# Layer 0's value projection: tile 0's values in front of tile 1's turning, and two engines kept in source order

## The chip, the cores and the metric

The kernel runs on one core of one Trainium2 chip. The metric is the device time of one execution in microseconds (us). Before the change it is 2489.64 us, the median of three runs from 2487.28 to 2490.44.

The engines are called as in the profile: PE is the tensor engine, ACT is ScalarE, DVE is VectorE, POOL is GpSimd, SP is the engine that issues the DMAs.

## The reference

A decoder trunk of two layers over 1024 tokens of width 1024, in float32: layer 0 mixes with native sparse attention (NSA), layer 1 with forgetting attention over shared keys and values. Each layer also attends to 256 memory tokens and ends with a gated convolutional FFN. What matters here is how layer 0 begins:

```python
def rms_norm(x, g):
    xf = x.astype(jnp.float32)
    y = xf * lax.rsqrt(jnp.mean(xf * xf, axis=-1, keepdims=True) + EPS)
    return (y * g.astype(jnp.float32)).astype(x.dtype)
...
h = rms_norm(x, attn_norm[l])
...
proj = h @ w_in
q = proj[..., :MIX_W].reshape(B, S, N_MIX_HEADS, HEAD_DIM)
kv = proj[..., MIX_W:MIX_W + BRANCH_KV_W].reshape(B, S, 6, N_KV_GROUPS, HEAD_DIM)
gate_logit = proj[..., MIX_W + BRANCH_KV_W:MIX_W + BRANCH_KV_W + GATE_W]
...
gates = jax.nn.sigmoid(gate_logit + gate_b).reshape(B, S, N_MIX_HEADS, 3)
```

The rows of x are normalized, and of their projection two value blocks (128 columns each) and the 36 gate columns are made first: 292 columns in all.

## The kernel before

Every float32 operand of a matmul is split into a high and a low half, and each product is made of three matmuls, high by high, high by low and low by high (`mm3`, lines 171 to 173). The halves are made by `split`: the high half by an ACT copy (line 86), the low half by a DVE subtraction (line 92).

`layer0_proj` holds the first part of layer 0. The 1024 tokens are 8 tiles of 128 rows. A tile goes through these steps:

- `load_x` (line 1183): a DMA of the 512 KB tile `xl`, into one of two buffers.
- `norm_x`: ACT squares the rows and sums them (line 132, it writes into `xn`), ACT makes the mean (line 127, `ss`), POOL the power -1/2 (line 135, `rs`), DVE the product with the gain `gb` (line 149, `xn`, two buffers).
- `norm_turn`: PE turns (transposes) eight blocks of 128x128 into two PSUM tiles `psb` (line 164), and both are split into `hT` (lines 86 and 92).
- the values: 24 matmuls of 292 columns over the 8 blocks of the depth (lines 171 to 173) into one `psb`, out of `hT` and the split weights `wh` and `wl`, of which there are four pairs with two depth blocks each. The fourth pair's raw weights `wr` have to wait for one of three buffers.
- `store_v`: the 256 value columns are split into `sv` (line 86 on ACT, line 92 on DVE) and stored to DRAM (line 272). DVE adds the gate bias (line 1203).

PSUM gives four `psb` tiles, shared by the turning and the values. Behind the eight tiles ACT makes the sigmoid of the gates (line 1204), and PE goes on to the projections of keys and queries, the compression of the keys and the memory tokens' keys and values, in an order that a string of letters sets.

A scheduler of the framework sets each engine's order: of the instructions whose inputs it believes ready it takes the one with the best priority, by estimates of its own. Under `tc.manual_schedule(engines=...)` the named engines keep the order in which the code issues the block's instructions, and instructions from outside the block can still go between. In the loop before, no engine is under it: the code norms and turns tile t+1 ahead of the values of tile t, and the scheduler orders all engines. On each engine the instructions then run strictly in the order of its queue.

Of the kernel before, what the change touches and what calls it, by code (L numbers as in the profile page):

```python
# [17 lines left out]
P = 128  # L18
D = 1024
S = 1024  # L20
NT = S // P
# [23 lines left out]
class Trunk:  # L45
# [1120 lines left out]
    def layer0_proj(self, cpool):  # L1166
        nc, a, tc = self.nc, self.a, self.tc
        w = a["a_w_in"][0]
        self.mem = []
        self.qd0 = self.dp.tile([2, 2, NH * 32, S], F32, name="qd0")  # L1170
        self.kd0 = self.dp.tile([2, 2, 4 * 32, S], F32, name="kd0")
        self.vd0 = self.dp.tile([S, 4, 2 * HD], F32, name="vd0")
        self.qm0 = self.dp.tile([2, NMH * HD, S], F32, name="qm0")
        self.gates = cpool.tile([P, NT, NH * 3], F32, name="gates")
        self.kc = cpool.tile([P, NG, 64], F32R, name="kc")
        self.vc = cpool.tile([P, NG, 2, HD], F32R, name="vc")
        with tc.tile_pool(name="l0p", bufs=1) as pool:
            h = [self.hpair() for _ in range(2)]
            xs = []

            def load_x(t):
                xs.append(self.sb(pool, [P, D], F32, "xl", 2))
                nc.sync.dma_start(xs[t], a["x"][0, t * P:(t + 1) * P, :])

            def norm(t):
                self.norm_t(pool, xs[t], gb, h[t // 4][0], h[t // 4][1], (t % 4) * P)
            load_x(0)
            gb = self.gain(pool, a["attn_norm"][0:1, :], 2)
            wv = self.load_block(w, [(1152, 128), (1408, 164)])
            gbias = pool.tile([P, NH * 3], F32, name="gbias")  # L1190
            nc.sync.dma_start(gbias, a["a_gate_b"].to_broadcast([P, NH * 3]))
            norm(0)
            for t in range(NT):
                if t + 1 < NT:
                    load_x(t + 1)
                    norm(t + 1)
                ps = self.psb()[:, 0:292]
                hh, hl = h[t // 4]
                o = (t % 4) * P
                for kt in range(KT):  # L1200
                    self.mm3(ps, (hh[:, kt, o:o + P], hl[:, kt, o:o + P]), wv(kt, 0, 292), kt == 0, kt == KT - 1)
                self.store_v(pool, ps[:, 0:256], self.vd0[t * P:(t + 1) * P], 4)
                nc.vector.tensor_tensor(self.gates[:, t, :], ps[:, 256:292], gbias, ALU.add)
            nc.scalar.activation(self.gates, self.gates, AF.Sigmoid)
            g0 = self.gates.rearrange("p t (h b) -> p t h b", b=3)[:, 0, :, 0]
            nc.vector.tensor_scalar(g0, g0, self.rv, None, ALU.mult)
            self.masks(pool, cpool)
            ct = pool.tile([P, 2, 32], F32, name="ct")
            nc.sync.dma_start(ct, a["rope_cmp"])
            comp = [self.compress(pool, h, w, kind, ct) for kind in range(2)]  # L1210
            mems = [self.mem_kv(pool, l) for l in range(2)]
            keys = self.rope_proj(cpool, h, w, [(1024, 128), (1280, 128)], self.kd0, 0, None)
            first = self.rope_proj(cpool, h, w, [(0, 256)], self.qd0, 0, QSC)
            order = "k cc kkk m kkk dd kkkk m kkk c kkk m d q m c q m c q m d q m d q n c q n d q n c q n d qq n qq n q n qqqqqq"
            gens = {"k": keys, "q": first, "c": comp[0], "d": comp[1], "m": mems[0], "n": mems[1]}
            for name in order.replace(" ", ""):
                next(gens[name], None)
            for g in (comp[0], comp[1], mems[0], mems[1], first):
                for _ in g:
                    pass  # L1220
        return h
# [1224 lines left out]
```

## Time and profile before

| | us |
|---|---|
| median of three runs | 2489.64 |
| the profiled execution | 2489.81 |
| its span | 2487.7 |
| PE busy in it | 2424.5 |
| first turning of tile 0, from the span's start | 8.17 |
| first value matmul | 18.86 |
| first turning of tile 7 | 43.93 |
| first matmul of the key projection | 51.23 |

The span is the time from the first to the last instruction that the profile shows. A row of a timeline gives the start and the length of an instruction (or of several equal ones, with their count), its engine and line, what it writes and reads, and in brackets how long the engine had been idle and what it waited for. Lengths of matmuls overlap, because they are pipelined: the distance between two starts is what one costs.

### The profile page before, as it was taken

What the parts mean: (1) busy time and instruction counts of PE and PEld (TensorE: products, weight loads), DVE (VectorE), ACT (ScalarE), POOL (GpSimd) and SP (SyncE); (2) the same over time, 40 slices, a digit from 0 to 9 for tenths busy, and PEclk for the clock granted to TensorE, in tenths of its full rate; (3) what the DMA queues carried; (4) which work ended last, traced back from release to release, by engine and by line L of the source; (5) the groups of instructions that cost most, each with busy time, mean ns of one, the idle gap of its engine ahead of it and who ended that gap; (6) DMA issues with size and microseconds to landing.
All of it is one profiled execution on the core that took longest, in us unless ns stands there. A gap on an engine that the chain in (4) does not pass through costs nothing.

```text
span 2487.7 us, 35535 instructions
## 1 busy us (share of the span) xinstructions
PE 2424.5 (97%) x12210; PEld 2041.9 (82%) x12210; DVE 1897.2 (76%) x3143; ACT 1362.4 (55%) x2623; POOL 744.1 (30%) x620
## 2 busy tenths in 40 slices
PE   7999999998999999999999999999999999999998
PEld 7788888877878888888889988887777888888886
DVE  5757999894598888788666478878479788788765
ACT  5435989894454444454455257757254444454444
POOL 0114455454165545520000000001236545451000
PEclk9999999999999999999999999999999999999999
DMA  8465233255423333366336567666613323338523
GB/s 253 144 207 161 70 87 101 82 144 168 161 73 110 106 102 110 101 240 227 102 119 186 156 178 202 187 181 190 214 68 111 106 94 114 98 102 318 167 93 120
DMA packets 303276, 357.68 MB, mean 144 GB/s; under 512 B 38024, under 2 KB 183288, under 8 KB 303096
## 3 DMA queue, kind: packets, MB, share of 16 engines
q1 hardware_dynamic: 303096, 355.41, 45.2%
q8 instruction: 97, 1.59, 0.3%
q14 instruction: 83, 0.68, 0.1%
HBM read 245.55 MB, written 109.78 MB: 143 GB/s over the span
## 4 chain that ended last, share of the span: by engine, by line
PE 81%; DVE 8%; ACT 3%; issue 3%; DMA 2%; POOL 1%; SPq 0%; POOLq 0%; DVEq 0%; ACTq 0%
PE psb L171 16%; PE psb L172 16%; PE psb L173 16%; PE psa L171 6%; PE psa L173 6%; PE psa L172 6%; PE psa L321 5%; PE psb L453 5%; PE psb L480 5%; DVE wl L92 1%; DVE hT L92 1%; DVE pt L467 1%; ACT ps L381 1%; ACT pt L464 1%; DVE ps L361 1%
## 5 line engine op out<-in xcount | busy, mean ns | idle before, releaser
L2056 DVE SCALAR_TENSOR_TENSOR v<-u,cw,v 128x1023 f32<-128x1023 f32 (+1 forms) x176 | 288.8, 1642 | 64.1 <-ACT v L2054 64.0
L92 DVE TENSOR_TENSOR wl<-wr,wh 128x512 fp32r<-128x512 f32 (+2 forms) x244 | 233.4, 961 | 117.6 <-ACT wh L86 117.1
L86 ACT ACTIVATE wh<-wr 128x512 fp32r<-128x512 f32 (+2 forms) x244 | 182.2, 751 | 241.4 <-PE psa L173 109.8
L171 PE MATMUL psb<-hT,wh 128*128 128x512 f32 x736 | 293.1, 398 | 0.4 <-DVE pt L467 0.4
L467 DVE TENSOR_TENSOR pt<-psb,pt 128x512 fp32r<-128x512 f32 (+2 forms) x380 | 247.5, 660 | 60.3 <-ACT pt L464 58.0
L173 PE MATMUL psb<-hT,wl 128*128 128x512 f32 x736 | 287.8, 391 | 0.0
L172 PE MATMUL psb<-hT,wh 128*128 128x512 f32 x736 | 287.6, 391 | 0.0
L464 ACT ACTIVATE pt<-psb 128x512 fp32r<-128x512 f32 (+2 forms) x380 | 216.1, 575 | 95.1 <-PE psb L453 91.9
L2054 ACT ACTIVATE v<-u,cw 128x1024 f32<-128x1024 f32 x88 | 109.6, 1246 | 285.2 <-DVE u L2043 273.8
L480 PE MATMUL psb<-pt,vv 128*128 128x512 f32 (+2 forms) x864 | 221.1, 356 | 5.6 <-DVE pt L467 4.7
L321 PE MATMUL psa<-kk,qq 128*128 128x512 f32 (+4 forms) x792 | 176.3, 340 | 5.0 <-ACT pm L378 3.0
L381 ACT ACTIVATE ps<-ps,stat 128x640 f32<-128x640 f32 (+4 forms) x192 | 147.8, 774 | 28.2 <-DVE stat L361 27.9
L173 PEld LDWEIGHTS psb<-hT,wl 128*128 128x128 f32 x736 | 138.3, 188 | 29.3
L135 POOL TENSOR_TENSOR rs<-ss,consts 128x1 f32<-128x1 f32 x24 | 17.3, 720 | 482.0 <-ACT ss L127 315.9
L171 PEld LDWEIGHTS psb<-hT,wh 128*128 128x128 f32 x736 | 138.5, 188 | 27.1 <-DVE pt L467 1.1
L172 PEld LDWEIGHTS psb<-hT,wh 128*128 128x128 f32 x736 | 138.6, 188 | 25.1
L453 PE MATMUL psb<-consts,ps 128*128 128x128 f32 x928 | 146.9, 276 | 7.3 <-DVE ps L419 2.8
L480 PEld LDWEIGHTS psb<-pt,vv 128*128 128x128 f32 x864 | 137.4, 192 | 19.7 <-DVE pt L467 7.5
L361 DVE CUSTOM_DVE_ANT_0 ps<-psa,caub 128x128 f32<-128x128 f32 (+1 forms) x192 | 139.7, 751 | 15.6 <-PE psa L321 13.8
L544 POOL TENSOR_TENSOR wr<-wr 128x512 f32<-128x512 f32 x16 | 21.8, 1368 | 408.6 <-DVE stat L361 240.4
L321 PEld LDWEIGHTS psa<-kk,qq 128*128 128x128 f32 x792 | 121.5, 189 | 24.3 <-DVE stat L361 5.3
L453 PEld LDWEIGHTS psb<-consts,ps 128*128 128x128 f32 x928 | 110.4, 142 | 34.0 <-DVE ps L419 4.6
(327 smaller groups left out, 6647.3 us busy)
## 6 DMA issues: line engine op xcount, KB each, us to landing
wr<-in_w_up_dram SPq DMA_DIRECT2D x88, 512.0 KB
wr<-gd SPq DMA_DIRECT2D x154, 256.0 KB
gd<-v SPq DMA_DIRECT2D x88, 256.0 KB
o<-ob SPq DMA_DIRECT2D x128, 128.0 KB
wr<-o SPq DMA_DIRECT2D x32, 512.0 KB
hT<-in_w_down_dram SPq DMA_DIRECT2D x64, 256.0 KB
gd<-gs SPq DMA_DIRECT2D x60, 256.0 KB
qd<-st SPq DMA_DIRECT2D x56, 256.0 KB
```

Source lines behind the costliest of these rows:

```text
L86: self.nc.scalar.activation(hi, src, AF.Copy)
L92: self.nc.vector.tensor_tensor(lo, src, f32(hi), ALU.subtract)
L171: mm(out, lh, rh, start=first, stop=False, skip_group_check=more)
L172: mm(out, lh, rl, start=False, stop=False, skip_group_check=more)
L173: mm(out, ll, rh, start=False, stop=last, skip_group_check=more)
L321: nc.tensor.matmul(out, w, rhs, start=b not in banks[:i], stop=b not in banks[i + 1:])
L381: nc.scalar.activation(p, p, AF.Exp, bias=st[:, 0, ii:ii + 1], scale=-1.0, accum_out=st[:, 1, ii:ii + 1])
L453: nc.tensor.transpose(tp[0:kb, x:x + P], br["pt"][ii][:, o:o + kb], self.ident)
L464: nc.scalar.activation(st["hi"], st["src"], AF.Copy)
L467: self.nc.vector.tensor_tensor(st["lo"], st["src"], f32(st["hi"]), ALU.subtract)
L480: self.nc.tensor.matmul(out, v, t, start=st["begin"] and i == 0, stop=st["end"] and i == len(mms) - 1)
L2056: nc.vector.scalar_tensor_tensor(v[:, d:], u[:, :S - d], cw[:, tap, i:i + 1], v[:, d:], ALU.mult, ALU.add)
```

## The change

The norm and the turning of a tile become two calls, and the loop is written out anew: tile 0 is turned, tile 1 is normed, tile 0's values are made, and only then tile 1 is turned. For tiles 2 to 7, tile t is loaded, normed and turned, and then the values of tile t-1 are made. The whole stands under `manual_schedule` for PE and ACT. DVE, POOL and SP stay with the scheduler.

```diff
-            def norm(t):
-                self.norm_t(pool, xs[t], gb, h[t // 4][0], h[t // 4][1], (t % 4) * P)
             load_x(0)
...
-            norm(0)
-            for t in range(NT):
-                if t + 1 < NT:
-                    load_x(t + 1)
-                    norm(t + 1)
+            def turn(t, xn):
+                self.norm_turn(xn, h[t // 4][0], h[t // 4][1], (t % 4) * P)
+
+            def values(t):
                 ps = self.psb()[:, 0:292]
...
+            with tc.manual_schedule(engines={mybir.EngineType.PE, mybir.EngineType.Activation}):
+                turn(0, self.norm_x(pool, xs[0], gb))
+                load_x(1)
+                xn = self.norm_x(pool, xs[1], gb)
+                values(0)
+                turn(1, xn)
+                for t in range(2, NT):
+                    load_x(t)
+                    turn(t, self.norm_x(pool, xs[t], gb))
+                    values(t - 1)
+                values(NT - 1)
```

PE at the start of the program, before. `xn_129` holds the normed rows of tile 0, `xn_152` those of tile 1; `psb_173` takes the values of tile 0:

```order
L164 MATMUL psb_136<-consts,xn_129 128x128 x4
L164 MATMUL psb_143<-consts,xn_129 128x128 x4
L164 MATMUL psb_159<-consts,xn_152 128x128 x4
L164 MATMUL psb_166<-consts,xn_152 128x128 x4
L171 MATMUL psb_173<-wh_102,hT_91 128x292
L172 MATMUL psb_173<-wl_103,hT_91 128x292
```

PE at the same place, after. `xn_131`, `xn_154` and `xn_207` are tiles 0, 1 and 2; `psb_161` takes the values of tile 0, `psb_228` those of tile 1:

```order
L164 MATMUL psb_138<-consts,xn_131 128x128 x4
L164 MATMUL psb_145<-consts,xn_131 128x128 x4
L171 MATMUL psb_161<-wh_102,hT_91 128x292
L172 MATMUL psb_161<-wl_103,hT_91 128x292
...
L173 MATMUL psb_161<-wh_123,hT_92 128x292
L164 MATMUL psb_191<-consts,xn_154 128x128 x4
L164 MATMUL psb_198<-consts,xn_154 128x128 x4
L164 MATMUL psb_214<-consts,xn_207 128x128 x4
L164 MATMUL psb_221<-consts,xn_207 128x128 x4
L171 MATMUL psb_228<-wh_102,hT_91 128x292
```

The 24 value matmuls of tile 0 moved ahead of the turning of tile 1. From the turning of tile 2 on, PE has the same sequence as before.

ACT in the rounds of tiles 1 to 3, before. `xn_258` and `xn_311` are the squares of tiles 3 and 4, `psb_159` and `psb_212` are turned blocks of tiles 1 and 2, and `sv_198` is the eviction of tile 0's values:

```order
L86 ACTIVATE hT_91<-psb_159 128x4x128
L86 ACTIVATE hT_91<-psb_166 128x4x128
L132 ACTIVATE xn_258,ss_259<-xl_256 128x1024
L127 ACTIVATE ss_259<-ss_259,eps 128x1
L86 ACTIVATE sv_198<-psb_173 128x4x64
L86 ACTIVATE hT_91<-psb_212 128x4x128
L86 ACTIVATE hT_91<-psb_219 128x4x128
L132 ACTIVATE xn_311,ss_312<-xl_309 128x1024
L127 ACTIVATE ss_312<-ss_312,eps 128x1
L86 ACTIVATE sv_251<-psb_226 128x4x64
```

ACT at the same place, after. `xn_207` and `xn_260` are the squares of tiles 2 and 3, `psb_191` and `psb_214` are turned blocks of tiles 1 and 2, and `sv_186` and `sv_253` are the evictions of the values of tiles 0 and 1:

```order
L86 ACTIVATE sv_186<-psb_161 128x4x64
L86 ACTIVATE hT_91<-psb_191 128x4x128
L86 ACTIVATE hT_91<-psb_198 128x4x128
L132 ACTIVATE xn_207,ss_208<-xl_205 128x1024
L127 ACTIVATE ss_208<-ss_208,eps 128x1
L86 ACTIVATE hT_91<-psb_214 128x4x128
L86 ACTIVATE hT_91<-psb_221 128x4x128
L86 ACTIVATE sv_253<-psb_228 128x4x64
L132 ACTIVATE xn_260,ss_261<-xl_258 128x1024
L127 ACTIVATE ss_261<-ss_261,eps 128x1
```

Before, the square of tile t+3 stands ahead of the eviction of tile t's values. After, the square of tile t+2 stands behind it.

On DVE the product of tile 1 moves ahead of the fourth weight's low half, and each later product behind the value eviction and gate sum of its round. On SP the tile loads and the value stores change places with each other and with loads of constants. On ACT, a square of a memory tile (line 132) stands between tile 7's square and its mean. POOL has its instructions in the same order as before, and behind the value stage PE, ACT and DVE do too.

## The prediction

> **What bounds the kernel now.** I read the page's first part, then who waited for whom on TensorE (PE) by stretches of the span, then the timeline of the first 60 us, since the change touches nothing behind it.
>
> ```profile
> span 2487.7 us, 35535 instructions
> PE 2424.5 (97%) x12210; PEld 2041.9 (82%) x12210; DVE 1897.2 (76%) x3143; ACT 1362.4 (55%) x2623; POOL 744.1 (30%) x620
> ```
>
> PE is the bound: 63 us of the span are not its own. The waits of PE between 0 and 60 us (line waited for: us in total, times, longest):
>
> ```profile
> PE psb L164 <- DVE xn L149: 15.3, 2, 8.2
> ```
>
> That is the first tile's normalized rows (8.2 us, before anything can run) and the second tile's (7.1 us). The timeline shows the second wait (start us, us, engine, line, out<-in):
>
> ```profile
> 8.17 1.97 PE L164 MATMUL psb<-consts,xn 128*128 128x128 f32 x8 [8.17 <-DVE xn L149]
> 9.94 1.07 ACT L86 ACTIVATE hT<-psb 128x512 fp32r<-128x512 f32 x2
> 10.75 1.28 DVE L92 TENSOR_TENSOR hT<-psb,hT 128x512 fp32r<-128x512 f32 x2
> 10.89 1.06 ACT L132 ACTIVATE xn<-xl 128x1024 f32<-128x1024 f32 x1
> 12.72 1.06 ACT L132 ACTIVATE xn<-xl 128x1024 f32<-128x1024 f32 x1 [0.68 <-DMA xl<-in_x_dram]
> 13.97 0.69 ACT L86 ACTIVATE wh<-wr 128x584 fp32r<-128x584 f32 x1
> 14.56 0.46 ACT L127 ACTIVATE ss<-ss,eps 128x1 f32<-128x1 f32 x2
> 14.69 0.77 DVE L92 TENSOR_TENSOR wl<-wr,wh 128x584 fp32r<-128x584 f32 x1 [2.66 <-ACT wh L86]
> 15.90 2.48 DVE L149 SCALAR_TENSOR_TENSOR xn<-xl,rs,gb 128x1024 f32<-128x1024 f32 x2 [0.45 <-POOL rs L135]
> 17.24 1.97 PE L164 MATMUL psb<-consts,xn 128*128 128x128 f32 x8 [7.10 <-DVE xn L149]
> 18.86 0.59 PE L171 MATMUL psb<-wh,hT 128*128 128x292 f32 x1
> ```
>
> Tile 0 is turned (transposed) by 10.14 and its halves are split by 12.03, yet its value matmuls start at 18.86, because the turning of tile 1 stands ahead of them. From then on PE doesn't stop. One round of this steady state, with two value matmuls at the slow start ahead of it:
>
> ```profile
> 19.74 0.45 PE L171 MATMUL psb<-wh,hT 128*128 128x292 f32 x1
> 19.98 0.44 PE L172 MATMUL psb<-wl,hT 128*128 128x292 f32 x1
> ...
> 20.62 1.06 ACT L132 ACTIVATE xn<-xl 128x1024 f32<-128x1024 f32 x1 [0.78 <-DVE hT L92]
> 21.80 0.29 ACT L127 ACTIVATE ss<-ss,eps 128x1 f32<-128x1 f32 x1
> 22.18 0.55 POOL L135 TENSOR_TENSOR rs<-ss,consts 128x1 f32<-128x1 f32 x1 [5.79 <-ACT ss L127]
> 22.76 1.28 DVE L149 SCALAR_TENSOR_TENSOR xn<-xl,rs,gb 128x1024 f32<-128x1024 f32 x1 [2.19 <-POOL rs L135]
> 23.20 0.30 PE L172 MATMUL psb<-wl,hT 128*128 128x292 f32 x1
> 23.33 0.30 PE L173 MATMUL psb<-wh,hT 128*128 128x292 f32 x1
> 23.47 1.04 PE L164 MATMUL psb<-consts,xn 128*128 128x128 f32 x8
> 23.67 0.39 ACT L86 ACTIVATE sv<-psb 128x256 fp32r<-128x256 f32 x1 [1.57 <-PE psb L173]
> 24.10 1.09 ACT L86 ACTIVATE hT<-psb 128x512 fp32r<-128x512 f32 x2
> 25.08 1.06 ACT L132 ACTIVATE xn<-xl 128x1024 f32<-128x1024 f32 x1
> 27.55 1.04 PE L164 MATMUL psb<-consts,xn 128*128 128x128 f32 x8
> ```
>
> A round is 4.08 us (23.47 to 27.55): 8 turnings and 24 value matmuls back to back. The next tile's norm is a chain over four engines: square on ScalarE (20.62), mean, power on GpSimd, product on VectorE, ready at 24.04. It costs PE nothing only because the square starts 2.7 us before PE's last value matmul (23.33).
>
> The stage's end, tile 7's turning and the first matmul of the key projection:
>
> ```profile
> 43.93 1.04 PE L164 MATMUL psb<-consts,xn 128*128 128x128 f32 x8
> 51.23 0.39 PE L171 MATMUL psb<-hT,wh 128*128 128x512 f32 x1
> ```
>
> **The change part by part.** The instructions behind this stage keep their order on every compute engine, so the question is how far 51.23 moves.
>
> *Start.* Tile 0's values now go ahead of tile 1's turning. Their third matmul needs the first low half, at 10.75 + 0.64 = 11.4. From there the spacing is 0.24 us (19.74 to 19.98) until the clock rises, then 0.13 (23.20 to 23.33). With a rise at 14.9 (grid below), 17 are issued by then. The seventh block needs the last weight's low half, at 14.69 + 0.77 = 15.46, and the last of 24 goes out at about 16.2. ScalarE squares tile 1 at 10.89 as before and no longer lets tile 2's square go between, so its rows are there at 10.89 + 3.48 = 14.4 and its turning follows without a gap, over at 17.1. So the 7.1 us go. What is late next is tile 2: its square stands behind the two eviction halves of tile 1 (high half at 16.9, the square 0.98 later as 24.10 to 25.08, so 17.9). Chain length, square to first turning: 20.62 to 24.04 plus 0.06, 3.48 us. So tile 2 is turned at 21.4 instead of 23.47: a gain of 2.1. Without the rise at 14.9 it is 22.6, a gain of 0.9.
>
> *Rounds.* In source order ScalarE has, per round, the two hT halves, the values' eviction sv, and only then the next square. The sv waits for the round's last value matmul; PE's next instruction, the next turning, waits for the chain behind that square. So each round's chain lies bare: sv starts 0.20 after PE could go on (23.47 to 23.67), holds ScalarE 0.43 (23.67 to 24.10), and the chain takes 3.48: 4.11 us of stall in each of the five rounds from tile 2's turning to tile 7's, 20.6 us. Queued behind the sv on ScalarE are the square and all that PE will do next; nothing else on PE may go ahead. Against 0 from a reason that the order excludes (square ahead of sv), 4.11 is the figure.
>
> *Extra squares.* In front of tile 7's mean there is now a memory tile's square, today at:
>
> ```profile
> 42.78 1.06 ACT L132 ACTIVATE xn<-xl 128x1024 f32<-128x1024 f32 x1 [0.58 <-DMA xl<-in_mem_dram]
> ```
>
> With its accumulator read it is 1.2 us more, once; a small weight split ahead of tile 4's mean adds 0.2.
>
> *Other queues.* The last two value blocks and the key weights' splits keep their order, so the 7.3 us from tile 7's turning to 51.23 stay. On SP the tile loads move behind value stores and small constants. A load took up to 5.4 us from issue to use:
>
> ```profile
> 24.07 0.33 SPq L1183 DMA_DIRECT2D xl<-in_x_dram  x1
> ...
> 29.49 1.06 ACT L132 ACTIVATE xn<-xl 128x1024 f32<-128x1024 f32 x1 [0.21 <-DMA xl<-in_x_dram]
> ```
>
> It is issued when the product two tiles earlier frees the buffer, over 12 us ahead of its square in the longer rounds (8.19 + 4.5): hidden, 0; the memory tile's load has some 6 us and could cost 1. VectorE and GpSimd only follow.
>
> *Clock.* At full clock the sum is -2.1 + 20.6 + 1.4 = +19.9. But PE stalls of this length have a price. Stretches of 3.41 us (PE busy, instructions, granted clock, DMA):
>
> ```profile
> 100.27:103.68 3.41, 1.99 (x14) 1.00 0.25 82
> 103.68:107.10 3.42, 3.42 (x22) 1.00 1.06 370
> ...
> 110.51:113.92 3.41, 1.40 (x12) 1.00 0.90 281
> 113.92:117.33 3.41, 2.55 (x12) 0.50 0.56 158
> 117.33:120.75 3.42, 3.42 (x16) 0.50 0.86 224
> ...
> 1745.49:1748.90 3.41, 1.47 (x7) 1.00 0.28 67
> 1748.90:1752.32 3.42, 3.39 (x10) 0.50 0.53 155
> ```
>
> The clock changes on a grid of 3.41 us: after a stretch with 1.40 or 1.47 us of work it was halved, after 1.99 it was not; it came back after a stretch that was busy throughout, not after 2.55. (On the same grid 21.76 is an edge, where the spacing fell from 0.24 to 0.13; the column reads 1.00 before that too, so at the start the spacing is the witness.) A stall of 4.11 us, cut by the grid anywhere, leaves one stretch with under 1.4 us of work. So the clock is halved in each of the six stalls, and comes back one or two stretches into the work. Half of 3.41 is 1.7 us: 10.2 us if one stretch of each of six rounds is lost, 20.5 if two. At about 8.2 + 1.7 a round is close to three stretches (10.24), so the phase hardly drifts and one stretch is the usual price; I take seven, 12 us.
>
> The Trainium skill ("TensorE: Matmul & The Clock Gate", "What's actually happening") says that the clock halves only after at least one idle window of about 3.4 us on a free-running grid. By that rule a stall of 4.11 holds a whole window about one time in five, and the sum would be some +23. The trace differs: 1.40 us of work in 3.41 was little enough, so I keep 12.
>
> Sum: 2489.81 (the profiled execution, 0.2 over the median of 2489.64) + 19.9 + 12 = 2521.7, say 2522.
>
> **Rivals.**
>
> 1. *The clock stays full* in most or all rounds (0.12): the same stalls and no halving, 2489.8 + 19.9 = 2510. For it: 1.99 us of work in a stretch was enough. Against it: a stall leaves less. The Trainium skill's rule above would put the time near this end.
>
> 2. *The delay is made up later* (0.10). PE's waits between 60 and 400 us:
>
> ```profile
> PE psb L172 <- DVE wl L92: 5.1, 2, 2.9
> ```
>
> If these weight halves came earlier against a delayed PE, 5.1 us and the halved stretches behind them (6.83 / 2 = 3.4) would go: +23.5, 2513. Against it: VectorE, which makes them, is itself fed by PE's projections, so it is delayed too. A shift at 51 us otherwise goes through to the end.
>
> 3. *Only the start counts, and the kernel is faster* (0.03): place, the first stall; mechanism, tile 2's norm runs while tile 0's values do and every later norm stays hidden. Tile 2 would be turned at 17.2, a gain of 6.3: 2483.5. It decides if a round's stall is under 1 us. The raw tile 2 is there at 12.72, which speaks for it; the order of ScalarE speaks against it.
>
> 4. *Nothing measurable* (0.03): a round stalls by well under 1 us and the start's gain pays for it, 2490.
>
> **How the numbers follow.** My forecast, bare chains with the clock halved in each round, has 0.72: 2522, from 2489.8 + 19.9 + 10 - 3 (a start or a later wait that goes my way) to 2489.8 + 19.9 + 20.5. The range reaches down to rival 1, and some way below it for a little of rival 2, up to 2530: 2508 to 2530. About 0.2% (5 us) is what a measurement of this kernel can tell from no change. Faster has 0.03 (rival 3), same 0.03 (rival 4), slower 0.94.
>
> **What would show it.** In the changed kernel's timeline: tile 0's values at about 11.4, tile 2's turning near 21.4, rounds of 9.5 to 11.5 us instead of 4.08, the wait of L164 on xn with seven entries instead of two and about 35 us in all, ScalarE's square right behind each sv, matmul spacing of 0.24 after each stall, and the key projection's first matmul at 80 to 86 instead of 51.23. The forecast is wrong if a square stands in the trace before the round's last value matmul, if the spacing stays at 0.13 after the stalls (then 2510), or if the time behind the first key matmul, 2436 us today, shrinks by more than 4.

## The result and the profile after

The changed kernel takes 2522.56 us (median of four runs, 2518.26 to 2526.56) against 2490.04 of the kernel before (2487.28 to 2493.78): a ratio of 1.0128, with an interval from 1.0116 to 1.0140. It is slower by about 32 us. Ratios here and below leave out the few executions in which the chip was disturbed.

The first part of the page (the profiled execution took 2521.09 us):

```profile
span 2519.2 us, 35528 instructions
PE 2436.5 (97%) x12210; PEld 2051.0 (81%) x12210; DVE 1892.6 (75%) x3143; ACT 1362.0 (54%) x2623; POOL 746.9 (30%) x620
```

PE's busy time grew by 12 us with the same instructions: they ran slower. The other 20 us of the longer span are idle. The waits of PE in the first 90 us:

```profile
PE psb L164 <- DVE xn L149: 24.5, 6, 4.8
PE psb L164 <- DMA wr<-in_a_w_in_dram: 8.6, 1, 8.6
```

The second row is the wait for tile 0, as before. In the first row six waits for the normed rows, of tiles 2 to 7, stand where there was one of 7.1 us for tile 1. The timeline of the start and of one round:

```profile
10.71 0.61 PE L171 MATMUL psb<-wh,hT 128*128 128x292 f32 x1
...
17.04 1.03 PE L164 MATMUL psb<-consts,xn 128*128 128x128 f32 x8
...
22.21 1.06 PE L164 MATMUL psb<-consts,xn 128*128 128x128 f32 x8 [4.14 <-DVE xn L149]
...
27.74 0.29 PE L173 MATMUL psb<-wh,hT 128*128 128x292 f32 x1
28.07 0.38 ACT L86 ACTIVATE sv<-psb 128x256 fp32r<-128x256 f32 x1 [4.11 <-PE psb L173]
28.35 1.05 ACT L132 ACTIVATE xn<-xl 128x1024 f32<-128x1024 f32 x1
...
29.89 0.55 POOL L135 TENSOR_TENSOR rs<-ss,consts 128x1 f32<-128x1 f32 x1 [9.15 <-ACT ss L127]
30.48 1.29 DVE L149 SCALAR_TENSOR_TENSOR xn<-xl,rs,gb 128x1024 f32<-128x1024 f32 x1 [1.47 <-POOL rs L135]
31.91 0.88 PE L164 MATMUL psb<-consts,xn 128*128 128x128 f32 x3 [3.88 <-DVE xn L149]
...
83.19 0.40 PE L171 MATMUL psb<-hT,wh 128*128 128x512 f32 x1
```

Tile 0's values start at 10.71 instead of 18.86, and tile 1 is turned at 17.04 without a wait. Then the square of tile 3 (28.35) stands right behind the eviction sv (28.07), which waited for PE's last value matmul (27.74), and PE waits for the whole chain until 31.91. (The view ended at 32.5 us, so that this row counts only three of the eight matmuls.) The key projection starts at 83.19 instead of 51.23, 32.0 us later. From there to the end of the span it is 2436.0 us (2519.2 - 83.19) against 2436.5. Between versions this remainder differs by more than that: it was 2432.2 to 2440.1 us in the profiles of this document.

The granted clock in stretches of 3.41 us, cut at the edges at which it changes here (PE busy, instructions, granted clock, DMA share and GB/s):

```profile
16.58:19.99 3.41, 1.49 (x13) 1.00 0.76 239
19.99:23.40 3.41, 1.19 (x11) 1.00 1.00 297
23.40:26.82 3.42, 3.42 (x17) 0.50 0.97 277
26.82:30.23 3.41, 1.21 (x9) 1.00 0.56 35
30.23:33.64 3.41, 1.73 (x9) 0.50 0.92 202
...
37.06:40.47 3.41, 1.50 (x11) 1.00 0.14 37
40.47:43.88 3.41, 1.39 (x7) 0.50 0.40 104
...
50.71:54.12 3.41, 1.25 (x11) 1.00 0.36 108
54.12:57.54 3.42, 3.42 (x16) 0.50 0.30 122
57.54:60.95 3.41, 1.15 (x9) 1.00 0.15 59
60.95:64.36 3.41, 1.80 (x9) 0.50 0.30 90
...
67.78:71.19 3.41, 1.46 (x11) 1.00 0.06 22
71.19:74.60 3.41, 0.59 (x3) 0.50 0.14 55
```

After each of the six stalls a stretch or two run at half the clock. No stretch here is without work, and still the clock was halved six times.

### The profile page after: what moved, and what is told of

Read it like the earlier page. It is cut to its first block, busy times and chain, and to the rows that moved or that the text cites. A ratio compares the mean times of both kernels' runs of the same rounds, so it can differ in the third digit from the quotient of the medians.

```text
span 2519.2 us, 35528 instructions
## 1 busy us (share of the span) xinstructions
PE 2436.5 (97%) x12210; PEld 2051.0 (81%) x12210; DVE 1892.6 (75%) x3143; ACT 1362.0 (54%) x2623; POOL 746.9 (30%) x620
## 4 chain that ended last, share of the span: by engine, by line
PE 81%; DVE 8%; issue 4%; ACT 3%; DMA 2%; POOL 1%; SPq 0%; POOLq 0%; DVEq 0%; ACTq 0%
PE psb L171 16%; PE psb L173 16%; PE psb L172 16%; PE psa L171 6%; PE psa L172 6%; PE psa L173 6%; PE psa L321 5%; PE psb L480 5%; PE psb L453 5%; DVE hT L92 1%; DVE wl L92 1%; DVE pt L467 1%; ACT ps L381 1%; ACT pt L464 1%; DVE ps L361 1%
```

## The experiments

The theory: in source order ScalarE's square stands behind the eviction of the values, so that PE waits for the whole norm in each round, and these waits halve PE's clock. The rivals: the new order on PE, or a fixed order as such, costs the time.

### ScalarE free again

```diff
-            with tc.manual_schedule(engines={mybir.EngineType.PE, mybir.EngineType.Activation}):
+            if True:
```

> The changed loop (tile 0's values in front of tile 1's turning) without the manual order: PE's queue is row for row that of the changed kernel, only ScalarE's differs (squares stand ahead of the value evictions again). Theory (bare chain behind the eviction on ScalarE): all the loss goes and the start's gain stays; tile 2 is turned at about 17, rounds are 4.1 us, the key projection starts near 45 to 48, total 2483 to 2488. Rival (the new PE order itself costs the time): total near 2522. Rival (the gain at the start is taken back by the tile loads, which come late when rounds are short): 2490.

It took 2492.43 us (11 runs), a ratio of 1.0016 (1.0008 to 1.0025). Some turnings, and the key projection:

```profile
18.55 1.06 PE L164 MATMUL psb<-consts,xn 128*128 128x128 f32 x8 [0.19 <-DVE xn L149]
24.17 1.06 PE L164 MATMUL psb<-consts,xn 128*128 128x128 f32 x8 [1.20 <-DVE xn L149]
...
44.80 1.06 PE L164 MATMUL psb<-consts,xn 128*128 128x128 f32 x8 [1.72 <-DVE xn L149]
52.12 0.40 PE L171 MATMUL psb<-hT,wh 128*128 128x512 f32 x1
```

These are tiles 2, 3 and 7. A row of ScalarE, the square of tile 7:

```profile
40.13 1.06 ACT L132 ACTIVATE xn<-xl 128x1024 f32<-128x1024 f32 x1 [3.65 <-DMA xl<-in_x_dram]
```

With the same queue on PE in this stage, some 28 of the 32 us are gone (the ratio leaves 4): PE's order is not the cause, and what has changed is the order on ScalarE and, behind it, on VectorE. The gain at the start is there, tile 2 is turned at 18.55 instead of 23.47, but it is lost again: the rounds are 4.1 to 6.0 us. Several squares wait for their tile's load, that of tile 4 for 1.73 us and that of tile 7 for 3.65 us, and these two hold up the hT halves that stand behind them. So the rival of the late loads has a part in it.

### The old loop in source order

```diff
             with tc.manual_schedule(engines={mybir.EngineType.PE, mybir.EngineType.Activation}):
                 turn(0, self.norm_x(pool, xs[0], gb))
-                load_x(1)
...
+                for t in range(NT):
+                    if t + 1 < NT:
+                        load_x(t + 1)
+                        turn(t + 1, self.norm_x(pool, xs[t + 1], gb))
+                    values(t)
```

> The old loop (tile 1 turned ahead of tile 0's values), but with PE and ScalarE in source order. Theory: the same bare chain in every round, and tile 2's turning comes one values block later than in the changed kernel, so about 3 to 5 us more than that: 2524 to 2530. Rival (moving the values is what costs): near 2490.

It took 2525.92 us (4 runs), a ratio of 1.0141 (1.0127 to 1.0155).

```profile
24.70 1.51 PE L164 MATMUL psb<-consts,xn 128*128 128x128 f32 x8 [3.88 <-DVE xn L149]
34.42 1.07 PE L164 MATMUL psb<-consts,xn 128*128 128x128 f32 x8 [3.88 <-DVE xn L149]
...
84.95 0.39 PE L171 MATMUL psb<-hT,wh 128*128 128x512 f32 x1
```

The same 3.88 us of wait and rounds of 9.7 to 11.5 us stand here without the values moved. So the move of the values is not the cause; by itself it is worth some 2 us in this stage (tile 2's turning at 22.21 against 24.70, the key projection at 83.19 against 84.95). The intervals of the two total times overlap.

### Filling the stalls

```diff
                     load_x(t)
+                    fill(26)
                     turn(t, self.norm_x(pool, xs[t], gb))
```

`fill(n)` makes n matmuls of 292 columns out of operands that are there, into a PSUM tile that nothing reads.

> The changed kernel with 26 idle matmuls of 292 columns put into each of the six stalls (3.5 us at full clock; their results are read by nothing, the work of the kernel is whole). The stalls stay, only the clock has no idle stretch. Theory: the halved clock cost 13 us, so 2507 to 2513, with spacing 0.13 in all rounds and rounds of about 8.2 us. Rival (the length of the rounds has nothing to do with the clock, or the filler delays the turning): 2522 or more.

The ratio is 1.0096 (1.0080 to 1.0111), with runs of 2509.66, 2515.25 and 2515.53 us. For its profile the same kernel ran again:

> The version with 26 idle matmuls in each stall once more, for its profile. Theory: spacing 0.13 in every round, no halved stretch before 80 us, rounds of 8.2 to 8.4 us, key projection at 70 to 73. If the filler itself were the limit, the wait of the turning on the product would be gone and rounds would be longer than 8.5. Total 2509 to 2516.

2516.03 us (4 runs), a ratio of 1.0105 (1.0087 to 1.0123). Turnings of tiles 2 to 6, and a row of ScalarE:

```profile
22.37 1.06 PE L164 MATMUL psb<-consts,xn 128*128 128x128 f32 x8 [0.66 <-DVE xn L149]
30.52 1.06 PE L164 MATMUL psb<-consts,xn 128*128 128x128 f32 x8 [0.40 <-DVE xn L149]
42.61 1.94 PE L164 MATMUL psb<-consts,xn 128*128 128x128 f32 x8 [4.34 <-DVE xn L149]
53.11 1.07 PE L164 MATMUL psb<-consts,xn 128*128 128x128 f32 x8 [0.41 <-DVE xn L149]
61.28 1.06 PE L164 MATMUL psb<-consts,xn 128*128 128x128 f32 x8 [0.41 <-DVE xn L149]
```

```profile
38.57 0.31 ACT L86 ACTIVATE cw2s<-cw 128x128 fp32r<-128x128 f32 x1 [6.30 <-DMA cw<-in_a_cmp_w_dram]
```

The two undisturbed filled rounds are 8.15 us (22.37 to 30.52) and 8.17 (53.11 to 61.28). The four rounds of the changed kernel from tile 2 to tile 6 were 9.7 to 10.6, 10.1 on the average (22.21 and 62.56 are 40.35 apart). So the halved clock was 1.9 us of a round, and the rest over the 4.1 of work, another 4.1, is the bare chain. The stage didn't come down to 70 to 73 as I expected (77.66), and the medians lie above the expected ranges, because one stall went wrong: the scheduler had put a small weight split of another stage into ScalarE's queue, ahead of the eviction, and ScalarE stood 6.30 us for its load. That round took 12.1 us (30.52 to 42.61), and the next, at the halved clock, 10.5.

### Half filled

The same with `fill(13)`, a single run.

> The changed kernel with 13 idle matmuls (1.75 us at full clock) in each of the six stalls, so that some 2.3 us of each stall stay empty. It tells how much emptiness halves the clock. If a stretch of 3.41 us with under about 1.5 us of work is enough, the stalls that fall whole into one stretch halve it (some 2 or 3 of six), the others don't, and the stage takes 3 to 8 us less than in the changed kernel (key projection at 75 to 80, total 2514 to 2520). If it takes a stretch with no work at all, no stall halves it and the key projection is at 70 to 73; if any gap of 2 us does, all six are halved and it is at 82 to 84.

2511.83 us, beside 2489.28 of the kernel before. The key projection started at 77.37. Stretches around four of the six stalls:

```profile
20.40:23.81 3.41, 1.54 (x13) 1.00 1.00 302
...
27.22:30.64 3.42, 1.29 (x10) 1.00 0.72 40
30.64:34.05 3.41, 3.41 (x17) 0.50 0.90 251
...
57.94:61.35 3.41, 1.71 (x15) 1.00 0.30 105
...
64.77:68.18 3.41, 0.88 (x7) 1.00 0.20 77
68.18:71.59 3.41, 2.91 (x13) 0.50 0.59 209
```

After 1.54 and 1.71 us of work the full clock stayed; after 1.29 and 0.88 it was halved. Four of the six stalls halved it, and in these six the boundary lies between 1.29 and 1.54 us. That is nearest to the first of the three theories, which had put it at two or three stalls and the total at 2514 or more. With 26 matmuls in each stall the stage took as much time (77.66), because there the late load took back what the clock gave.

### The eviction on VectorE

```diff
-                self.store_v(pool, ps[:, 0:256], self.vd0[t * P:(t + 1) * P], 4)
+                st = self.sb(pool, [P, 4, 2, HD], F32R, "sv", 2)
+                v = ps[:, 0:256].rearrange("p (h d) -> p h d", d=HD)
+                nc.vector.tensor_copy(st[:, :, 0, :], v)
+                self.lower(v, st[:, :, 0, :], st[:, :, 1, :])
```

The store behind it stays the same.

> The changed kernel, source order kept on PE and ScalarE, but the high half of the value eviction is copied by VectorE, so that nothing in ScalarE's queue waits for the values any more. Theory: then the square follows the hT halves at once; a round is 1.65 us (turning to square) plus the chain of 3.5, 5.1 to 5.3 us, with stalls of about 1 us, too short to halve the clock: key projection at 54 to 57, total 2492 to 2499. Rival (the loss is in PE's order or in source order as such, not in this one wait): stays at 2515 to 2525.

2494.81 us (10 runs), a ratio of 1.0018 (1.0008 to 1.0028).

```profile
33.61 1.06 PE L164 MATMUL psb<-consts,xn 128*128 128x128 f32 x8 [0.93 <-DVE xn L149]
38.81 1.06 PE L164 MATMUL psb<-consts,xn 128*128 128x128 f32 x8 [0.93 <-DVE xn L149]
...
56.59 0.40 PE L171 MATMUL psb<-hT,wh 128*128 128x512 f32 x1
```

Source order on both engines stays, and one instruction of each tile leaves ScalarE's queue. From tile 3's turning on the rounds fall to 5.2 us, as worked out, and some 28 of 32 us go. It is this one wait. (Tile 2 still waits 4.13 us, since its square stands behind the halves of tile 1 as before.)

### Squares one and two tiles ahead

Source order as in the change, but `norm_x` of a later tile is called ahead of the values: for tile t+1 (one ahead) or for tile t+2 (two ahead), right behind the turning of tile t. The edit for two ahead, where `norm(t)` loads and norms tile t:

```diff
+                norm(1)
+                norm(2)
                 values(0)
...
+                for t in range(1, NT):
+                    turn(t, xn[t])
+                    if t + 2 < NT:
+                        norm(t + 2)
+                    if t > 1:
+                        values(t - 1)
```

> As the version that norms two tiles ahead, but only one tile ahead: the square of tile t+1 stands behind the hT halves of tile t and ahead of the values' eviction. Theory: the chain of 3.5 us starts 1.65 us into a round, so rounds are 5.1 to 5.2 us instead of 4.08, tile 2's turning near 17.5, key projection near 51, total 2488 to 2495. Rival (any square ahead of the eviction hides the chain fully): rounds of 4.08 and the same time as two tiles ahead, 2490.

One ahead took 2491.67 us (10 runs), a ratio of 1.0007 (0.9997 to 1.0018):

```profile
29.03 1.06 PE L164 MATMUL psb<-consts,xn 128*128 128x128 f32 x8 [0.94 <-DVE xn L149]
34.24 1.06 PE L164 MATMUL psb<-consts,xn 128*128 128x128 f32 x8 [0.94 <-DVE xn L149]
...
52.03 0.47 PE L171 MATMUL psb<-hT,wh 128*128 128x512 f32 x1
```

Rounds of 5.21 us: the chain starts behind the hT halves, and with these it is 1 us longer than the 4.1 us of work that hide it.

> The changed kernel's PE order, PE and ScalarE still in source order, but the code norms tile t+2 right after tile t is turned, ahead of the values of tile t-1. Theory: source order as such costs nothing; with the squares two tiles ahead no chain is bare: 2483 to 2488, like the version without the manual order. Rival (a fixed order on two engines costs by itself, since it can't follow what is ready): 2495 to 2525.

Two ahead took 2490.85 us (12 runs), a ratio of 1.0008 (0.9999 to 1.0017). PE's rows, then one of ScalarE:

```profile
21.98 1.04 PE L164 MATMUL psb<-consts,xn 128*128 128x128 f32 x8
...
38.36 1.04 PE L164 MATMUL psb<-consts,xn 128*128 128x128 f32 x8
...
50.21 0.40 PE L171 MATMUL psb<-hT,wh 128*128 128x512 f32 x1
```

```profile
41.41 1.06 ACT L132 ACTIVATE xn<-xl 128x1024 f32<-128x1024 f32 x1 [4.53 <-DMA xl<-in_mem_dram]
```

The rounds are 4.1 us, and tile 7 is turned at 38.36, 5.6 us earlier than in the kernel before: a fixed order costs nothing as such. But the total is that of before (the profiled execution, 2484.27 us, is the fastest of the twelve). ScalarE stood 4.5 us at a memory tile's square, which the scheduler had put in front of tile 7's halves and whose load was late; PE had to wait for these, and of the 5.6 us only 1.0 was left at the key projection.

### The memory tiles loaded early

Two ahead, and the gain and the two tiles of the first memory layer loaded into buffers of their own while tiles 5 and 6 are normed.

```diff
+                    if t in (5, 6):
+                        self.pre.append(self.sb(pool, [P, D], F32, "xm", 2))
+                        nc.sync.dma_start(self.pre[-1], a["mem"][0, (t - 5) * P:(t - 4) * P, :])
```

> Two tiles ahead in source order, and the first memory layer's gain and two tiles are loaded early into buffers of their own, so that the memory square, which the scheduler puts into ScalarE's queue ahead of tile 7's halves, no longer waits 4.5 us for its load. Theory: the last stall (2.3 us on PE and a halved stretch) goes, key projection at 45 to 47 instead of 50.2, total 2484 to 2488. Rival (the early loads only push the key weights back, and PE waits for these instead): key projection at 49 to 52 and total 2488 to 2493.

2490.01 us (12 runs), a ratio of 1.0000 (0.9991 to 1.0008).

```profile
47.31 0.50 PE L171 MATMUL psb<-hT,wh 128*128 128x512 f32 x1 [0.74 <-ACT wh L86]
49.51 0.50 PE L173 MATMUL psb<-hT,wl 128*128 128x512 f32 x1 [1.46 <-DVE wl L92]
```

```profile
45.98 0.31 ACT L86 ACTIVATE cw2s<-cw 128x128 fp32r<-128x128 f32 x1 [4.14 <-DMA cw<-in_a_cmp_w_dram]
```

The key projection starts 3.9 us before that of the kernel before, and waits 2.2 us there for its weights' halves. The loads of these weights now stand behind the memory tiles, but they are not what PE waits for: the last of the four was issued at 31.21, and ScalarE splits the weights from 46.64 on without waiting for a load. It came to them so late because it had stood 4.14 us at the small weight split, whose load was issued at 42.95. So the rival's total fits, but its cause does not; one foreign instruction has taken the place of another. Behind the 2.2 us of waits comes a stretch at half the clock (50.45 to 53.86), and at the next turning, that of the first memory tile, 1.1 of the 3.9 us are left (67.28 against 68.34). What takes these by the end of the run stays open; no version here beats the kernel before.

## Why the prediction was right

| term | predicted, us | measured, us |
|---|---|---|
| tile 2's turning | 21.4, a gain of 2.1 | 22.21, a gain of 1.3 |
| five bare chains and the extra squares | +22.0 | five times 4.1, by the filled rounds, and 0.9 more ahead of tile 7 (a wait of 4.77 instead of 3.88): +21.4 |
| halved clock | +12 | 1.9 a round, by the two undisturbed filled rounds, times six: +11.4 |
| behind the key projection | 0 | -0.5 |

The sum of the right column is +31.0; the spans differ by 31.5.

- *Start.* Right in kind, 0.8 late: tile 0 came 0.4 later in this execution, and the clock rose at 16.58 instead of 14.9, since the grid of stretches lies differently in each execution (the edges 21.76 before and 16.58 after are not a whole number of stretches apart).
- *Rounds.* 9.7 to 11.5 us, as expected. The bare chain as the cause is shown from three sides: without the fixed order, under the same order on PE, the loss goes (ratio 1.0016); it goes with the one eviction taken from ScalarE's queue (1.0018); and it stands in full in the old loop, once that is in source order (1.0141).
- *Clock.* Rival 1 is out: all six stalls halved it. I took seven halved stretches, one a round as a rule. There were ten, two in each of four rounds, some of them partly empty of work, so that the price came out near that of seven: the size is partly luck. The Trainium skill ("TensorE: Matmul & The Clock Gate", "What's actually happening") asks for an idle window. The trace differs: the stalls left 1.15 to 1.50 us of work in the stretch, and the clock was halved all the same.
- *Rival 2*, that the delay is made up later, is out. Between 92 and 432 us (the stretch from 60 to 400, moved by 32) PE still waits 5.4 us for those weight halves, where it waited 5.1 before, and the delay is 32.0 us at the key projection and 31.5 at the end. (That the two agree so closely is luck, given a remainder that differs by up to 8 us between versions.)
- *Rival 3*, that only the start counts, is not borne out even where the later norms are hidden: two tiles ahead, 5.6 us of gain were there at tile 7, and none in the total.

The expectations that missed were above all those on the repaired versions: I reckoned 2483 to 2488, from the gain at the start, and three of them came out at 2490 to 2492. I had left out the foreign instructions in ScalarE's queue and, for the version without a fixed order, that the squares come to wait for their tiles' loads. The filled versions missed their totals too, the full one upward and the half one downward.

## What to carry to other kernels

A square, a copy or any first step of the next round's chain belongs ahead of an instruction that waits for this round's end, on an engine that works strictly in order; writing the code tile by tile and then fixing source order puts it behind. Count the chain against a round: 3.5 us of norm behind 0.6 us of waiting cost 4.1 us where a round has 4.1 us of work, and nothing if it starts two tiles ahead. When an engine's order is fixed, look also at what the scheduler still puts between, and at the loads that these instructions wait for.

## What was not expected of the hardware

- *A partly idle stretch halves PE's clock.* In the stalls of the changed and the half filled kernel it was halved after 0.88 to 1.50 us of work in 3.41 us, and not after 1.54 or 1.71, and once not after 1.49. That is no sharp boundary: further on it was halved after 1.60 and 1.70 us in the kernel before (stretches from 581.55 and 1697.71) and after 1.84 us in the version without a fixed order (from 501.31). Nor is there one for the way back: the full clock came back after 2.91 us of work (half filled), but not after 2.55 in the kernel before and 3.12 in the version without a fixed order (from 504.72). What else decides stays open.
- *Idle matmuls pay.* 26 matmuls whose results nobody reads cut a round from 10.1 to 8.2 us, because they kept the clock.
- *The spread between runs goes with the clock.* Of the runs of the kernel before beside the first experiments, the six with a mean granted clock of 0.995 took 2491.7 us on the average, the nine with 0.996 2488.9, the four with 0.997 2487.1, the two with 0.998 2487.2, and the one with 0.999 2485.49. A difference of 0.004 is 10 us of the span's cycles, and the times differ by 6. So a gain of 5 us at the start is of the size of what the clock gives or takes later. That the lie of the grid, which differs in each execution, makes this difference is my reading, not shown.
